# A hybrid decoder layer in fp32 on one core: norm factors' transposes, attention's last splits and the splits of loaded operands one step later, silu's table and one weight's split sooner

## The chip, the core and the metric

The kernel runs on one core of one Trainium2 chip. A core has five engines with an instruction queue each: TensorE (PE in the profile), VectorE (DVE), ScalarE (ACT), GpSimdE (POOL) and SyncE (SP), which here issues all the DMAs. They meet through semaphores. The metric is the device time of one execution in microseconds. Before the change it is 2059.78 us, the median of three runs (2059.01 to 2061.59).

## What is computed

The reference is one decoder layer on an x of 1 x 2048 x 1024 in float32. Two token mixers work side by side on the same normalised input: gated linear attention (four heads of 64 by 128) and a gated short convolution. Their outputs are concatenated, projected and added to x. A SwiGLU feed-forward part (FFN, width 2816) and a last norm follow.

```python
h = rmsnorm(x, norm1_g[l])
proj = h @ w_in[l]
p_q, p_k, p_v, p_g, p_a, c_b, c_c, c_h = jnp.split(proj, splits, axis=-1)
...
log_a = jax.nn.log_sigmoid(p_a @ w_gate_up[l] + b_gate[l]) / GATE_NORMALIZER
o = gla_chunked(q, k, v, log_a)
o = rmsnorm(o, gla_norm_g[l])
o = o * jax.nn.silu(p_g.reshape(bsz, seq, GLA_HEADS, GLA_DV))
...
o_conv = c_b * causal_depthwise_conv(c_c * c_h, conv_w[l])
mixed = jnp.concatenate([o_gla, o_conv], axis=-1) @ w_out[l]
x = x + mixed
h2 = rmsnorm(x, norm2_g[l])
ffn = (jax.nn.silu(h2 @ w_ffn_gate[l]) * (h2 @ w_ffn_up[l])) @ w_ffn_down[l]
x = x + ffn
return rmsnorm(x, norm_f_g)
```

## The kernel before

**Precision.** A product of float32 matrices is made of three matmuls. Each operand is split into a rounded upper part, hi, and the rest, lo (split, L190: hi is a copy on ACT, lo a subtraction on DVE), and product_step (L455) issues hi x hi at L460, hi x lo at L461 and lo x hi at L462. Every weight and every moving operand therefore costs one instruction on ACT and one on DVE before PE can use it.

**Products.** The input projection and the FFN work with seven block products in place of eight (a Strassen-Winograd scheme). The list PRODUCTS (L48) pairs weight blocks with operand blocks: A11 B11, S1 T1, S2 T2, A12 B21, S3 T3, S4 B22, A22 T4. One call of unit (L464) takes one weight of 1024 x 256 and does the seven products, mul(0) to mul(6), on 1024 positions. A product is 12 matmuls with 512 columns. The accumulators oa and ob (PSUM banks) are used again within a unit: mul(4) adds to oa, after ACT has copied c12 out of it (L500); L489 adds a later accumulator to a copy, on DVE. Seven split quarters of a weight go through four buffers.

**Halves.** The 2048 positions are two halves of 1024. in_proj(0) and in_proj(1) make the input projection, a unit per two blocks of columns; out_proj(0) and out_proj(1) make the output projection (L1201 to L1204); ffn_up and ffn_down follow for each half. Everything between them goes through DRAM.

**Order.** The program is traced by Python generators. A product ends in tick (L271). On every second tick it takes one step of the generator that stands first in background (more often while hurry, steady or hasty hold), and on one of four ticks one step of ahead. So a generator's yields say after how many products its next piece is traced. The tile framework then plans each engine's instructions in an order of its own, from the order of tracing and from estimated times, and the engine takes them in that order. behind(marks) and tc.issue_after(instruction) hold an instruction behind given ones. In the opening, that is, in the first quarter of the input projection up to its first whole unit, ordered is set: split_in_order (L177) and queued (L167) chain the instructions of ACT, and those of DVE, in the order in which they are written, and ticks take no step.

**The opening's first unit.** unit_weights (L418) leaves A22 unsplit while ordered is set (L451). The unit splits it at L518, after the four subtractions of T4 and their splits (difference, L730, called by rest() in two portions through then()). After that the order by hand ends.

**Loaded operands.** load_pairs (L917) gets the second half's operands of the input projection for in_proj(1), four tiles for each of the seven blocks. Four blocks were stored split and are loaded as pairs (load_pair). T3, B22 and T4 (WHOLE, L59) were stored unsplit; load_whole (L923) loads such a tile and splits it at once. load_h2 and act_op use load_whole for the FFN.

**Norm factors.** position_rstd (L217) sums squares over partitions by matmuls, makes 1/sqrt on DVE by eleven small operations (L230, L243 to L248), copies it along the free axis (rep, L234) and transposes that four times on PE into a bank (L238). h2_ahead (L1278) calls it twice at the beginning of ffn_up(0), and finish_later (L1400) twice in the second half, both as steps of ahead. combine (L328) follows in h2_ahead, with 28 steps.

**Attention.** gla_half (L1056) does 16 chunks of 128 positions by three steps each: gla_scores, gla_finish of the chunk before, gla_outputs. gla_finish (L1157) transposes the normed output of a chunk, multiplies by the gate (L1162), splits it (L193, L194) and stores both parts in s_gla. out_proj loads these as operands (build_mix, L1185).

**Tables.** ACT loads a table of functions when an instruction needs another set. finish_rstd (L252), which h2_first uses in out_proj(1), takes Ln and Exp. silu (L538) in the FFN needs its own set.

Of the kernel before, what the change touches and what calls it, by code (L numbers as in the profile page):

```python
# [20 lines left out]
P = 128  # L21
# [32 lines left out]
def tile_hymba_block(ctx, tc, x, xt, win, wa, wgu, wout, wffn, wdown, wdown_first, small, out):  # L54
# [97 lines left out]

    last_hi, last_lo, raw_loads = [], [], []
    last_out = []
# [61 lines left out]

    def position_rstd(n, *sums, into=()):  # L217

# [16 lines left out]
        ]  # L235
        for dst in (rb, *into):
            for t in range(PT):
                pe.transpose(dst[:, t * P : (t + 1) * P], rep[:, t, :], ident[:])  # L238
        return rb

# [11 lines left out]
    def finish_rstd(v, tot, n, rb=None):  # L252
        l, y0 = bt("l"), bt("y0")
        act.activation(l[:], tot[:], AF.Ln, bias=eps[:], scale=1.0 / n)
        act.activation(y0[:], l[:], AF.Exp, scale=-0.5)
        dve.tensor_scalar(v[:], tot[:], 1.0 / n, EPS, ALU.mult, ALU.add)
        newton((v if rb is None else rb)[:], v[:], l[:], y0[:])
# [206 lines left out]
    def unit(src, ops, into=None, onto=None, raw=None, between=(), rest=None):  # L464
# [43 lines left out]
        mul(2, oa)  # L508
        c12 = copied("c12", oa, (0, 1))
        o = mul(3)  # L510
        then()
        plus(c11, o)
        mul(4, oa)
        then()
        plus(c22, oa)
        if rest is not None:
            next(rest, None)
            w["A22"] = weight_quarter(w["A22"])  # L518
            held[:] = last_hi + last_lo
            ordered.clear()  # L520
        mul(5, ob)
        plus(c12, ob)
        mul(6, oa)
        if into is not None or onto is not None:
            copied("c21", oa, (1, 0))
        return [(0, 0, c11, False), (1, 1, c22, False), (0, 1, c12, False), (1, 0, oa, True)]

    def settled(c, in_psum):
# [388 lines left out]
    def load_pairs(src):  # L917
        ops = no_operands()
        for _, n in PRODUCTS:
            ops[n] = [(load_whole if n in WHOLE else load_pair)(p) for p in src[n]]  # L920
        return ops

    def load_whole(src):  # L923

        o = opp.tile([P, 2, PB], F32R, name="op", tag="op")
        load(o[:, 1, :].bitcast(F32), src[:])
        split(o[:, 1, :].bitcast(F32), o[:, 0, :], o[:, 1, :])
        return o
# [127 lines left out]
    def gla_half(half):  # L1056
# [7 lines left out]
        for n, (b, t) in enumerate(chunks):  # L1064
            cur = nxt
            s = gla_scores(b, t, *cur)
            yield
            if o is not None:
                gla_finish(*chunks[n - 1], *o)
                yield  # L1070
            if n + 1 < len(chunks):
                nxt = gla_load(*chunks[n + 1])
            o = gla_outputs(b, t, *s)
            yield
        gla_finish(b, t, *o)
        done.add((b, t))
# [80 lines left out]
    def gla_finish(b, t, osb, g):  # L1157
# [4 lines left out]
        dve.scalar_tensor_tensor(osb[:], ot[:], col(C_GN), g[:], ALU.mult, ALU.mult)  # L1162
        split(osb[:], g[:].bitcast(F32R), osb[:].bitcast(F32R))
        for e, y in enumerate((g, osb)):
# [67 lines left out]
    def h2_first(ssq, ops):  # L1232
# [5 lines left out]
        for j in range(2):  # L1238
            rb.append(tiny.tile([P, PB], F32, name="rb2", tag="rb"))
            column_rstd(ssq[j], D, rb[j])  # L1240
            yield

        def put(n, k, h):
            if n in LATER:
# [33 lines left out]
    def h2_ahead(ssq):  # L1278
# [3 lines left out]
        for j in range(2):  # L1282
            for _ in range(2):
                yield
            rb.append(position_rstd(D, ssq[j]))

# [113 lines left out]
    def finish_later(half):  # L1400

        for j in range(2):
# [6 lines left out]
            yield  # L1409
            rb = position_rstd(D, ssq)  # L1410
            for d in range(KD):
                y = bt("y")
                load(y[:], s_x1[2 * half + j][d][:])
                yield
                dve.scalar_tensor_tensor(y[:], y[:], col(C_GF + d), rb[:], ALU.mult, ALU.mult)
                store(out[2 * half + j, :, d, :], y[:])
# [222 lines left out]
```

## Time and profile before

| what | value |
|---|---|
| median of three runs | 2059.78 us (2059.01 to 2061.59) |
| profiled execution, its own time | 2056.94 us |
| span of its instructions | 2055.2 us |
| mean granted TensorE clock | 0.995 |
| instructions | 27032 |
| matmuls | 9271 |
| DMA traffic | 422.54 MB, 206 GB/s on the mean |

All rows come from that one profiled execution. A row of the timeline has the start in us from the span's start, the duration, the engine, the line, the operation with its output and input, its shape, and in brackets the engine's idle time before it and what ended that. A matmul's duration is modelled, and matmuls overlap: how fast PE goes is read from one start to the next. A row of the windows has the stretch and its length, then the busy time and the count for PE, PEld (weight loads), DVE, ACT and POOL, the granted TensorE clock, the busy share of the DMA engines and GB/s. A row of the waits has the engine, the line that waits, what it waits for, and then the total, the number and the longest.

### The profile page before, as it was taken

The numbers are of one execution on the slowest core, as the hardware profiler recorded it, in microseconds if no ns is written. First come the engines' busy times: TensorE is split into PE (matmuls) and PEld (weight loads), VectorE is DVE, ScalarE is ACT, GpSimd is POOL, SyncE is SP. The second block draws the span as 40 slices with busy tenths as digits, with TensorE's granted clock in tenths as the row PEclk, the third lists the DMA queues.
The fourth block names the chain that finished last, engine by engine and source line by source line (L and its number), as shares of the span: only waits on it lengthen the run. The fifth ranks groups of instructions, "written<-read, shape, count | busy, mean of one in ns | idle before, by whom it ended". The sixth has DMA issues, their size and how long they took to land.

```text
span 2055.2 us, 27032 instructions
## 1 busy us (share of the span) xinstructions
PE 2024.1 (98%) x9271; PEld 1664.6 (81%) x9271; DVE 1548.4 (75%) x2533; ACT 979.9 (48%) x1934; POOL 336.4 (16%) x218
## 2 busy tenths in 40 slices
PE   9999999999999999999999999999999999999997
PEld 8778878787888888888888888887888878888886
DVE  7878976569743787887786788877777777778884
ACT  6665455766543344444444552335544544453344
POOL 0000000000002451232131112201312221211213
PEclk9999999999999999999999999999999999999999
DMA  7356786425686873555454676576544534486663
GB/s 261 116 196 214 281 303 194 140 75 170 221 275 218 327 273 123 207 182 205 159 181 147 236 277 253 190 279 249 180 148 169 188 125 169 168 323 215 241 226 117
DMA packets 189738, 422.54 MB, mean 206 GB/s; under 512 B 19904, under 2 KB 65184, under 8 KB 180128
## 3 DMA queue, kind: packets, MB, share of 16 engines
q1 hardware_dynamic: 189600, 420.81, 57.8%
q8 instruction: 73, 1.20, 0.2%
q14 instruction: 65, 0.53, 0.1%
HBM read 276.02 MB, written 144.70 MB: 205 GB/s over the span
## 4 chain that ended last, share of the span: by engine, by line
PE 86%; DVE 5%; DMA 4%; ACT 3%; issue 2%; SPq 0%; POOL 0%; DVEq 0%; ACTq 0%; POOLq 0%
PE mm L460 25%; PE mm L462 24%; PE mm L461 24%; DMA op<-sa_T 2%; PE mm L1201 2%; PE mm L1202 2%; PE mm L1204 2%; DVE wq L194 1%; DMA raw<-in_wffn_dram 1%; DVE h L882 1%; PE a_ps L958 1%; PE mm L744 1%; PE mm L746 1%; PE mm L745 1%; PE o_ps L1125 1%
## 5 line engine op out<-in xcount | busy, mean ns | idle before, releaser
L460 PE MATMUL mm<-op,wq 128*128 128x512 f32 x2467 | 961.7, 393 | 13.7 <-ACT c L500 6.6
L461 PE MATMUL mm<-op,wq 128*128 128x512 f32 x2467 | 960.8, 390 | 0.2 <-DVE op L194 0.2
L462 PE MATMUL mm<-op,wq 128*128 128x512 f32 x2467 | 951.2, 390 | 0.5 <-DVE wq L194 0.2
L193 ACT ACTIVATE wq<-raw 128x512 fp32r<-128x512 f32 (+2 forms) x612 | 355.4, 587 | 588.3 <-PE mm L462 456.5
L194 DVE TENSOR_TENSOR wq<-raw,wq 128x512 fp32r<-128x512 f32 (+2 forms) x612 | 449.1, 739 | 179.7 <-ACT wq L193 177.8
L460 PEld LDWEIGHTS mm<-op,wq 128*128 128x128 f32 x2467 | 464.2, 188 | 118.2 <-ACT c L500 8.5
L462 PEld LDWEIGHTS mm<-op,wq 128*128 128x128 f32 x2467 | 464.2, 188 | 100.1 <-DVE wq L194 2.4
L461 PEld LDWEIGHTS mm<-op,wq 128*128 128x128 f32 x2467 | 464.3, 188 | 96.1 <-DVE op L194 1.3
L1183 POOL TENSOR_TENSOR ssx<-ssx,q 128x512 f32<-128x512 f32 x52 | 74.8, 1453 | 867.6 <-ACT q L1182 867.4
L489 DVE TENSOR_TENSOR c<-mm,c 128x512 f32<-128x512 f32 x196 | 134.8, 688 | 56.2 <-PE mm L462 53.7
L489 DVE TENSOR_TENSOR y<-mm,y 128x512 f32<-128x512 f32 x185 | 126.5, 687 | 47.4 <-PE mm L462 47.1
L435 DVE TENSOR_TENSOR raw<-raw 128x512 f32<-128x512 f32 (+2 forms) x192 | 151.7, 794 | 3.2
L1314 POOL TENSOR_TENSOR t<-c,c 128x512 f32<-128x512 f32 x44 | 73.9, 1678 | 432.0 <-DVE c L1310 409.7
L500 ACT ACTIVATE c<-mm 128x512 f32<-128x512 f32 x198 | 115.5, 588 | 19.0 <-PE mm L462 15.8
L1201 PE MATMUL mm<-op,wq 128*128 128x512 f32 x256 | 100.7, 395 | 0.0
L435 DVE TENSOR_TENSOR s<-raw 128x512 f32<-128x512 f32 (+2 forms) x96 | 64.1, 668 | 48.3 <-DMA raw<-in_wffn_dram 23.7
L1202 PE MATMUL mm<-op,wq 128*128 128x512 f32 x256 | 99.9, 390 | 0.0
L193 ACT ACTIVATE wq<-s 128x512 fp32r<-128x512 f32 (+2 forms) x96 | 56.2, 586 | 88.9 <-PE mm L462 85.3
L1396 POOL TENSOR_TENSOR y<-x,y 128x512 f32<-128x512 f32 x32 | 58.3, 1823 | 229.8 <-DVE y L489 163.7
L1204 PE MATMUL mm<-op,wq 128*128 128x512 f32 x256 | 79.9, 390 | 0.0
L435 DVE TENSOR_TENSOR raw<-s,raw 128x512 f32<-128x512 f32 (+2 forms) x96 | 69.8, 727 | 1.9
L194 DVE TENSOR_TENSOR op<-op 128x512 fp32r<-128x512 f32 x94 | 62.0, 686 | 5.3 <-ACT op L193 5.0
(230 smaller groups left out, 1777.4 us busy)
## 6 DMA issues: line engine op xcount, KB each, us to landing
raw<-in_wffn_dram SPq DMA_DIRECT2D x44, 1024.0 KB, 6.1
sa_B<-so SPq DMA_DIRECT2D x47, 512.0 KB, 3.4
op<-sa_B SPq DMA_DIRECT2D x47, 512.0 KB, 7.1
raw<-in_win_dram SPq DMA_DIRECT2D x22, 1024.0 KB, 5.4
sa_T<-so SPq DMA_DIRECT2D x44, 512.0 KB, 4.2
op<-sa_T SPq DMA_DIRECT2D x44, 512.0 KB, 6.6
raw<-in_wdown_dram SPq DMA_DIRECT2D x24, 768.0 KB, 5.6
sx<-y SPq DMA_DIRECT2D x48, 256.0 KB, 4.2
```

The costliest lines, as they stand in the source:

```text
L193: last_hi[:] = [act.activation(hi, src, AF.Copy)]
L194: last_lo[:] = [dve.tensor_tensor(lo, src, hi.bitcast(F32), ALU.subtract)]
L435: dve.tensor_tensor(*args)
L460: pe.matmul(o[:], wh, xh, start=first and k == 0, stop=False, skip_group_check=True)
L461: pe.matmul(o[:], wh, xl, start=False, stop=False, skip_group_check=True)
L462: return pe.matmul(o[:], wl, xh, start=False, stop=k == n - 1, skip_group_check=True)
L489: last_plus[:] = [dve.tensor_tensor(t[:], o[:], t[:], ALU.add)]
L500: last_out[:] = [act.activation(t[:], o[:], AF.Copy)]
L1183: pool.tensor_tensor(ssq[:], ssq[:], q[:], ALU.add)
L1201: pe.matmul(o[e, j][:], wh, m[:, 0, :], start=k == 0, stop=False)
L1202: pe.matmul(o[e, j][:], wh, m[:, 1, :], start=False, stop=False)
L1204: pe.matmul(o[e, j][:], wl, ops[k][j][:, 0, :], start=False, stop=k == KD - 1)
```

## The change

Six edits.

- position_rstd becomes a generator. It yields between the copy along the free axis and the transposes, and appends its result to a list. h2_ahead yields once before it and once after it for each of its two calls (before: twice ahead of it). finish_later takes one step more per call.
- gla_finish becomes a generator too. It yields after the multiplication by the gate. The split, now held behind last_out and last_plus, and the two stores are traced with the next step. gla_half drops the yield that stood behind it; its last call gives one yield more than before.
- load_undivided loads without a split. load_pairs uses it for T3, B22 and T4 and notes the tiles. due(n) in unit splits such a block's four tiles, held behind last_out: T3 after product 3 has been added, B22 after product 4, T4 after product 5. In all other units due finds nothing.
- In the opening's first unit A22 is split after c12's copy, ahead of product 3 and of T4's four; at its old place the outstanding lo is issued.
- After h2_first's two norms the table of silu is loaded (held behind the last Exp).
- load_whole is load_undivided and a split, for the callers that are left.

```diff
-    def position_rstd(n, *sums, into=()):
+    def position_rstd(n, rbs, *sums):
...
-        for dst in (rb, *into):
-            for t in range(PT):
-                pe.transpose(dst[:, t * P : (t + 1) * P], rep[:, t, :], ident[:])
-        return rb
+        yield
+        for t in range(PT):
+            pe.transpose(rb[:, t * P : (t + 1) * P], rep[:, t, :], ident[:])
+        rbs.append(rb)
...
-        act.activation(y0[:], l[:], AF.Exp, scale=-0.5)
+        last_exp[:] = [act.activation(y0[:], l[:], AF.Exp, scale=-0.5)]
...
         c12 = copied("c12", oa, (0, 1))
+        if rest is not None:
+            w["A22"] = weight_quarter(w["A22"])
         o = mul(3)
         then()
         plus(c11, o)
+        due("T3")
         mul(4, oa)
         then()
         plus(c22, oa)
+        due("B22")
         if rest is not None:
             next(rest, None)
-            w["A22"] = weight_quarter(w["A22"])
+            catch_up()
             held[:] = last_hi + last_lo
             ordered.clear()
         mul(5, ob)
         plus(c12, ob)
+        due("T4")
         mul(6, oa)
...
+    undivided = {}
+
+    def due(n):
+        for o in undivided.pop(n, ()):
+            with behind(last_out):
+                split(o[:, 1, :].bitcast(F32), o[:, 0, :], o[:, 1, :])
...
-            ops[n] = [(load_whole if n in WHOLE else load_pair)(p) for p in src[n]]
+            ops[n] = [(load_undivided if n in WHOLE else load_pair)(p) for p in src[n]]
+            if n in WHOLE:
+                undivided[n] = ops[n]
         return ops
 
-    def load_whole(src):
-
+    def load_undivided(src):
         o = opp.tile([P, 2, PB], F32R, name="op", tag="op")
         load(o[:, 1, :].bitcast(F32), src[:])
+        return o
+
+    def load_whole(src):
+
+        o = load_undivided(src)
         split(o[:, 1, :].bitcast(F32), o[:, 0, :], o[:, 1, :])
         return o
...
             if o is not None:
-                gla_finish(*chunks[n - 1], *o)
-                yield
+                yield from gla_finish(*chunks[n - 1], *o)
...
-        gla_finish(b, t, *o)
+        yield from gla_finish(b, t, *o)
         done.add((b, t))
...
         dve.scalar_tensor_tensor(osb[:], ot[:], col(C_GN), g[:], ALU.mult, ALU.mult)
-        split(osb[:], g[:].bitcast(F32R), osb[:].bitcast(F32R))
+        yield
+        with behind(last_out + last_plus):
+            split(osb[:], g[:].bitcast(F32R), osb[:].bitcast(F32R))
...
+        with tc.issue_after(last_exp[0].ins):
+            act.preload_act_table_set("silu_and_others")
+
...
-            for _ in range(2):
-                yield
-            rb.append(position_rstd(D, ssq[j]))
+            yield
+            yield from position_rstd(D, rb, ssq[j])
+            yield
...
-            rb = position_rstd(D, ssq)
+            rb = []
+            yield from position_rstd(D, rb, ssq)
...
-                dve.scalar_tensor_tensor(y[:], y[:], col(C_GF + d), rb[:], ALU.mult, ALU.mult)
+                dve.scalar_tensor_tensor(y[:], y[:], col(C_GF + d), rb[0][:], ALU.mult, ALU.mult)
```

More of the change, by code (lines that the diff above doesn't have):

```diff
@@ L151, in store @@
         return nc.sync.dma_start(dst, src)
-    last_hi, last_lo, raw_loads = [], [], []
+    last_hi, last_lo, raw_loads, last_exp = [], [], [], []
     last_out = []
```

## The prediction, made before the changed kernel was run

> **What bounds the kernel now.** I read the busy times and the chain of waits first, then the waits of TensorE alone, then the timeline around each long one, then windows for the granted clock.
>
> ```profile
> span 2055.2 us, 27032 instructions
> PE 2024.1 (98%) x9271; PEld 1664.6 (81%) x9271; DVE 1548.4 (75%) x2533; ACT 979.9 (48%) x1934; POOL 336.4 (16%) x218
> ...
> PE 86%; DVE 5%; DMA 4%; ACT 3%; issue 2%; SPq 0%; POOL 0%; DVEq 0%; ACTq 0%; POOLq 0%
> ```
>
> PE is busy for 98% and carries 86% of the chain. No edit touches a matmul of a product, so only PE's waits, and what follows them, can be won.
>
> ```profile
> PE mm L460 <- ACT c L500: 6.6, 5, 2.1
> PE mm L460 <- ACT wq L193: 3.0, 3, 1.9
> PE rb_ps L238 <- DVE rep L234: 2.3, 1, 2.3
> PE mm L460 <- ACT wq L180: 1.9, 1, 1.9
> ```
>
> The columns are the total wait, how often, and the longest. These four groups hold 13.8 us in ten waits. That is all there is to win, beside what a wait does to the matmuls after it:
>
> ```profile
> 80.48 0.39 PE L461 MATMUL mm<-op,wq 128*128 128x512 f32 x1
> 80.71 0.39 PE L462 MATMUL mm<-op,wq 128*128 128x512 f32 x1
> 83.03 0.50 PE L460 MATMUL mm<-op,wq 128*128 128x512 f32 x1 [1.93 <-ACT wq L180]
> ...
> 126.10 0.50 PE L460 MATMUL mm<-op,wq 128*128 128x512 f32 x1 [1.85 <-ACT wq L193]
> ...
> 277.18 0.50 PE L460 MATMUL mm<-op,wq 128*128 128x512 f32 x1 [2.11 <-ACT c L500]
> ...
> 278.35 0.63 PE L461 MATMUL mm<-op,wq 128*128 128x512 f32 x1
> 278.78 0.63 PE L462 MATMUL mm<-op,wq 128*128 128x512 f32 x1
> ...
> 764.83 0.50 PE L460 MATMUL mm<-op,wq 128*128 128x512 f32 x1 [0.63 <-ACT wq L193]
> ...
> 1423.57 0.50 PE L460 MATMUL mm<-op,wq 128*128 128x512 f32 x1 [1.69 <-ACT c L500]
> ...
> 1688.06 1.12 PE L238 MATMUL rb_ps<-ident,rep 128*128 128x128 f32 x4 [2.27 <-DVE rep L234]
> ```
>
> The first column is the start. Starts lie 0.23 apart as a rule (80.48 to 80.71) but 0.43 apart after the wait of 2.11 (278.35 to 278.78). The windows have the granted clock third from the end:
>
> ```profile
> 80.00:90.00 10.00, 8.07 (x28) 5.83 (x27) 8.91 (x15) 8.30 (x17) 0.00 (x0) 0.83 0.65 219
> 90.00:100.00 10.00, 10.00 (x46) 8.27 (x45) 8.08 (x16) 9.89 (x23) 0.00 (x0) 1.00 0.56 201
> 275.00:285.00 10.00, 7.89 (x28) 6.29 (x28) 6.69 (x11) 5.61 (x11) 0.00 (x0) 0.83 1.00 367
> 700.00:710.00 10.00, 10.00 (x46) 8.29 (x45) 10.00 (x9) 2.31 (x4) 7.43 (x5) 1.00 0.88 297
> 1680.00:1690.00 10.00, 7.51 (x34) 6.06 (x33) 7.15 (x22) 2.82 (x5) 0.00 (x0) 0.89 0.38 149
> 1690.00:1700.00 10.00, 10.00 (x43) 8.17 (x42) 3.57 (x6) 2.87 (x5) 0.00 (x0) 0.94 0.14 53
> ```
>
> Each of the waits of 1.93, 2.11 and 2.27 us is followed by a low clock: (1 - 0.83) x 10 = 1.7 us lost at 80 and at 275, and (1 - 0.89) x 10 + (1 - 0.94) x 10 = 1.7 us at 1688. These three waits are dear, some 3.7 us each, and three edits of the change aim at them.
>
> **Step 1, the norm factors' transposes.** One of the four calls of position_rstd stalls PE: at 1688.06 its transposes stand in PE's order ahead of a product, and rep comes late.
>
> ```profile
> 1687.59 0.42 DVE L234 COPY rep<-py 128x512 f32<-128x512 f32 x1
> ```
>
> rep ends at 1687.59 + 0.42 = 1688.01, the last of a chain of small operations that stand between splits on DVE. The new yield puts the transposes one ahead step later. Such a step is taken every fourth product; a product is 12 matmuls at 0.2275, 2.73 us, so 10.9 us later. That is far more than the 2.27 us missing: the wait and its clock loss go, -2.3 - 1.7 = **-4.0**. The end that is worst here is 0 (the transposes are placed where they were). Nothing is added. What is behind the transposes is the scaling of stored rows, spread over hundreds of us; the second half's h2_ahead starts its 28 combining steps 8 products (22 us) later, and its operands are wanted only by the second half of the FFN.
>
> **Step 2, the undivided operands of in_proj(1).** At 277.18 PE waits for ACT's copy of c12, and ACT had splits in front of it:
>
> ```profile
> 272.83 1.27 ACT L193 ACTIVATE op<-op 128x512 fp32r<-128x512 f32 x2 [1.52 <-DMA op<-siT]
> ...
> 275.50 1.14 ACT L193 ACTIVATE op<-op 128x512 fp32r<-128x512 f32 x2
> 276.54 0.58 ACT L500 ACTIVATE c<-mm 128x512 f32<-128x512 f32 x1
> ...
> 281.43 0.63 ACT L193 ACTIVATE wq<-raw 128x512 fp32r<-128x512 f32 x1 [2.05 <-DMA raw<-in_win_dram]
> ```
>
> The new code holds the twelve splits (0.63 on ACT, 0.69 on DVE each) behind c12's copy. Without the four ahead of it the copy ends over 2 us sooner. The most that can come is the wait and its clock, -2.1 - 1.7 = -3.8. But the next unit's weights only land at 281.43 with the DMA share at 1.00, and its first product began 284.39 - (281.43 + 0.63) = 2.3 us behind their first split: PE can move ahead by no more before it meets them. I take **-2.3**, nearest to that row; ends -3.8 (the loads move up too) and 0 (the splits, now late, take the place of the copy).
>
> **Step 3, A22 in the opening's first unit.** At 83.03 PE waits for A22's hi, the last on ACT's hand-written order:
>
> ```profile
> 82.36 0.61 ACT L180 ACTIVATE wq<-raw 128x512 fp32r<-128x512 f32 x1
> ...
> 89.01 0.69 ACT L993 ACTIVATE g<-z,sml 128x512 f32<-128x512 f32 x1 [0.42 <-PE z L984]
> ...
> 81.70 1.48 DVE L184 TENSOR_TENSOR op<-h,op 128x512 fp32r<-128x512 f32 x2
> 83.10 0.69 DVE L184 TENSOR_TENSOR wq<-raw,wq 128x512 fp32r<-128x512 f32 x1
> ```
>
> Moved before T4's four, its lo (0.69) is now ahead of theirs on DVE, which is full there (81.70 to 83.79 without a gap). T4's last lo then ends near 83.18 + 0.69 = 83.9, where an unstalled last product (from 80.71 + 0.23 = 80.94, 10 matmuls on, 83.2) wants it: a rest of 0.65. So at most -(1.93 - 0.65) - 1.7 = -3.0. But ACT is at 8.30 and 9.89 of 10 in the two windows from 80 on, and the wait of 1.85 at 126.10 is again one for ACT: what PE wins it waits out there, except for the time in which ACT itself waits for PE, such as 0.42 at 89.01; I put all such gaps up to 126 at 1.0, an estimate from that one. I take **-1.0**; ends -3.0 and +0.7 (one more split in T4's way, all else given back).
>
> **Step 4, silu's table.**
>
> ```profile
> 771.17 1.28 ACT L540 ACT_TABLE_LOAD   x1
> 772.46 0.63 ACT L540 ACTIVATE c<-c 128x512 f32<-128x512 f32 x1
> ```
>
> This load of 1.28 us, the first before silu in the FFN, moves from there to the output projection, where ACT has 2.31 of 10 busy (700 to 710). The wait that stands nearest, 0.63 at 764.83, comes before the load of before, so little of it is on the path: **-0.3**, ends 0 and -1.28. The Trainium skill, ScalarE: Activation LUTs, What ACT_TABLE_LOAD costs, gives 2.66 us for a switch with its drain, by which the lower end would be -2.7. This trace doesn't agree: the next ACT instruction starts 1.29 us after the load does.
>
> **Step 5, attention's last splits.** The step count per chunk stays, but the two halves end one background step later (every second product: 5.5 us). Only the end of the second half can matter, since out_proj(1) loads what it stores:
>
> ```profile
> 648.30 0.52 SPq L151 DMA_DIRECT2D sgla<-osb  x1
> ...
> 653.29 4.71 SPq L148 DMA_DIRECT2D op<-sgla  x7
> ...
> 669.79 0.39 PE L1201 MATMUL mm<-op,wq 128*128 128x512 f32 x1
> ...
> 759.12 0.69 DVE L435 TENSOR_TENSOR s<-raw 128x512 f32<-128x512 f32 x1 [2.87 <-DMA raw<-in_wffn_dram]
> ```
>
> The stores move from 648.30 to 653.8, the loads behind them on SP's queue from 653.29 to about 657.4: +4.1, since other loads use some of the gap. The cover is this: the products that use them begin at 669.79, still 12.4 us behind the first load. Behind them come h2_first's loads and DVE's full stage (10.00 of 10 at 700), which ends in gaps that wait for a weight's DMA, 2.87 at 759.12; these take up most of a shift. I take **+0.5**; ends 0 and +4.1, if that cover is gone.
>
> What this step wins is time in which ACT waits for osb. None of the four groups of PE's waits names it, so it counts 0.
>
> **Sum.** -4.0 - 2.3 - 1.0 - 0.3 + 0.5 = -7.1, from the profiled execution's 2056.94 to 2049.8. That execution is 2.84 below the median of the runs (2059.78); taken from the median the forecast is **2052.7**. A measurement of this kernel tells 0.2%, 4.1 us, from no change: faster means under 2055.7, slower over 2063.9.
>
> **Rivals.**
> - All is kept: the opening's gain isn't waited out and the loads move up. -4.0 - 3.8 - 3.0 - 0.3 = -11.1, 2048.7. For it: three clock losses go. Against: the DMA row at 281.43 and ACT at 9.89.
> - Given back: steps 2 and 3 end in the next wait, and the lag of step 5 passes on whole: -4.0 - 0.3 + 4.1 = -0.2, 2059.6. For it: DVE at 10.00 of 10 behind the loads. Against: the 12.4 us between loads and products.
> - Slower: the held splits become a series in front of products 4, 5 and 6 of in_proj(1)'s first unit. They are written behind the addition that ends each product before, and DVE may take them in that order:
>
> ```profile
> 274.68 0.39 PE L462 MATMUL mm<-op,wq 128*128 128x512 f32 x1
> ...
> 275.11 0.69 DVE L489 TENSOR_TENSOR c<-mm,c 128x512 f32<-128x512 f32 x1 [0.28 <-PE mm L462]
> ```
>
> The addition starts 0.43 behind the last matmul's start, 0.20 behind the moment at which the next product would start. With its 0.69, a hi of 0.63 and a lo of 0.69 each of the three products waits 2.2, over the 1.93 from which a clock loss of 1.7 follows here: 3 x 3.9 = 11.7, less the 3.8 of before, +7.9 in place of -2.3, so 2052.7 + 2.3 + 7.9 = 2062.9. It decides as soon as the splits stand behind the additions; one late landing among them makes it slower by more than a measurement can miss. Against: the order that is held names c12's copy alone, and T3's loads land before the wait.
> - The change doesn't do what it says: the transposes come where they were in PE's order, because the engine orders are planned from estimates. Then step 1 is 0: -3.1, 2056.7. Against: four whole products lie between now.
> - No clock loss follows a wait as such. The Trainium skill, TensorE: Matmul & The Clock Gate, Part 1: The HAM clock gate, has the array throttled only after a whole idle window of about 3.4 us, in a window that runs freely. By that rule the waits here cost their own length, and removing them wins that alone. As a mechanism of this kernel: step 1 is -2.3, the sum -2.3 - 2.3 - 1.0 - 0.3 + 0.5 = -5.4, so 2054.4. The trace speaks against it: 0.83, 0.83 and 0.89 follow waits of 1.93, 2.11 and 2.27. For it: the wait of 1.85 at 126.10 and that of 1.69 at 1423.57 are followed by full spacing.
>
> **How the numbers follow.** The forecast has a chance of 0.40 (its own range 2050 to 2055.5), all kept 0.15, no clock loss 0.03, given back 0.20, the series 0.15, no move 0.07. Faster by over 0.2%: 0.40 + 0.15 + 0.03 = 0.58. Within 0.2%: no move 0.07, 0.14 of given back and 0.08 of the series, 0.29 in all. Slower: the rest of these two, 0.06 + 0.07 = 0.13, where more waits come on top. The range reaches down to 2047, all kept with 1.7 for one of the waits that I count as untouched, and up to 2063.5, which holds the series.
>
> **What would show it.** Step 1: no wait at the transposes of L238's successor near 1685, and clock 1.00 there. Step 2: c12's copy on ACT ahead of the splits near 275, and a clock of 1.00. Step 3: A22's split ahead of T4's four, a wait under 0.7 near 81, and a longer one near 124. Step 4: no table load near 771, and one in the output projection. Step 5: op<-sgla near 657, and the FFN's first product not later against the output projection's. Waits of 2 us at products 4 to 6 near 275 to 300, or loads of op<-sgla that end PE's waits from 670 on, would prove me wrong.

## The result and the profile after

The changed kernel takes 2055.81 us, the median of eleven runs (2050.15 to 2058.08), against 2059.76 for the kernel before (2058.80 to 2063.48). The ratio is 0.9979 with a 95% interval of 0.9971 to 0.9987: some 4.3 us faster. Run a second time beside other kernels it had 0.9968 (0.9957 to 0.9980). The forecast was 2052.7, and its bound for "faster" was 2055.7: the first median lies 0.1 us outside that bound, while the interval of the ratio is clear of 1.

The first lines of the page after:

```profile
span 2048.4 us, 26987 instructions
...
PE 2021.6 (99%) x9271; PEld 1662.2 (81%) x9271; DVE 1549.0 (76%) x2533; ACT 971.7 (47%) x1930; POOL 335.4 (16%) x218
...
PE 87%; DVE 4%; DMA 4%; ACT 2%; issue 1%; SPq 1%; POOL 0%; DVEq 0%; ACTq 0%; POOLq 0%
```

The work is the same. ACT has four instructions and 8 us fewer; the four are loads of tables (19 before, 15 after). The profiled execution took 2050.15 us, 5.7 below its median, and that of before 2056.94, 2.8 below. So the two profiles show where the time went but not by how much; a second profile of the same program stands beside it below. TensorE's waits after:

```profile
PE mm L460 <- ACT c L500: 5.0, 3, 3.0
PE mm L460 <- ACT op L193: 2.1, 1, 2.1
...
PE mm L460 <- ACT wq L193: 1.2, 3, 0.5
```

Two of the four groups of before are gone: the wait for rep, and that for A22's split. That for weights has lost its 1.85. Two waits over 2 us are left, in the timeline of PE:

```profile
80.65 0.39 PE L462 MATMUL mm<-op,wq 128*128 128x512 f32 x1
80.88 0.39 PE L460 MATMUL mm<-op,wq 128*128 128x512 f32 x1
...
273.03 0.51 PE L460 MATMUL mm<-op,wq 128*128 128x512 f32 x1 [2.10 <-ACT op L193]
...
476.19 0.53 PE L460 MATMUL mm<-op,wq 128*128 128x512 f32 x1 [3.01 <-ACT c L500]
```

Near 81 PE goes on without a gap. Near 273 the wait is as long as before, and only its releaser has another name: a split of T3 in place of c12's copy. The wait of 3.01 is new. It is for the 1826th matmul with 512 columns (counted from 0). The kernel before has no wait there, but one 48 matmuls, or four products, ahead of it, for the 1778th:

```profile
469.92 0.50 PE L460 MATMUL mm<-op,wq 128*128 128x512 f32 x1 [1.11 <-DVE c L489]
```

That wait is gone, and so is one of 1.83 near 401. The windows around the two waits that went:

```profile
80.00:90.00 10.00, 9.79 (x44) 7.79 (x43) 9.91 (x18) 6.50 (x15) 0.00 (x0) 1.00 0.35 140
1680.00:1690.00 10.00, 10.00 (x45) 8.26 (x44) 4.73 (x7) 3.97 (x8) 0.00 (x0) 1.00 0.16 61
1690.00:1700.00 10.00, 10.00 (x50) 8.42 (x49) 8.90 (x24) 3.60 (x8) 0.35 (x1) 1.00 0.45 158
```

The clock, 0.83, 0.89 and 0.94 there before, is 1.00.

All kernels here issue the same 8437 matmuls of 512 columns, so they can be compared by the start of the n-th of them (from 0), read from the traces (the last row is the span):

| matmul | place | before | after | difference | after, second profile | difference |
|---|---|---|---|---|---|---|
| 288 | end of the opening | 79.12 | 79.06 | -0.06 | 79.72 | +0.60 |
| 480 | in_proj(0) | 129.49 | 124.14 | -5.35 | 124.79 | -4.70 |
| 1248 | attention's first chunks | 317.62 | 312.24 | -5.38 | 315.19 | -2.43 |
| 1824 | ahead of the wait of 3 us | 481.85 | 472.56 | -9.29 | 475.64 | -6.21 |
| 1872 | behind it | 497.12 | 492.33 | -4.79 | 495.71 | -1.41 |
| 2400 | out_proj(0) | 648.03 | 644.99 | -3.04 | 649.23 | +1.20 |
| 5712 | FFN, second half | 1407.19 | 1406.17 | -1.02 | 1412.09 | +4.90 |
| 6912 | ahead of the transposes | 1684.72 | 1681.61 | -3.11 | 1687.49 | +2.77 |
| 7008 | behind them | 1710.90 | 1704.76 | -6.14 | 1710.64 | -0.26 |
| end | | 2055.2 | 2048.4 | -6.8 | 2053.8 | -1.4 |

The change wins about 5 us in the opening's first unit and 4 at the transposes: from matmul 6880 to 7008 the kernel before takes 34.74 us, the changed one 30.40 in both profiles. (The row of 6912 shows less, because the sums of squares that belong to the transposes stand ahead of it before the change and behind it after.) Between matmuls 480 and 2400, where attention runs beside the projection, it gives back 2.3 us in the one profile (-5.35 to -3.04) and 5.9 in the other. From 2400 to 5712 it loses another 2.0 and 3.7; 1.8 and 1.7 of that lie between matmuls 3900 and 4100, where two new waits stand, of 0.63 and 0.56 near 1010.

### The profile page after: what moved, and what is told of

The parts are those of the page before. It is cut to its first block, busy times and chain, and to the rows that moved or that the text cites. A ratio compares the mean times of both kernels' runs of the same rounds, so it can differ in the third digit from the quotient of the medians.

```text
span 2048.4 us, 26987 instructions
## 1 busy us (share of the span) xinstructions
PE 2021.6 (99%) x9271; PEld 1662.2 (81%) x9271; DVE 1549.0 (76%) x2533; ACT 971.7 (47%) x1930; POOL 335.4 (16%) x218
## 4 chain that ended last, share of the span: by engine, by line
PE 87%; DVE 4%; DMA 4%; ACT 2%; issue 1%; SPq 1%; POOL 0%; DVEq 0%; ACTq 0%; POOLq 0%
PE mm L460 25%; PE mm L462 25%; PE mm L461 25%; PE mm L1220 2%; PE mm L1221 2%; PE mm L1223 2%; DMA raw<-in_wffn_dram 1%; DVE wq L194 1%; DVE h L894 1%; PE a_ps L976 1%; PE mm L756 1%; PE mm L758 1%; PE mm L757 1%; DMA raw<-in_win_dram 1%; PE o_ps L1144 1%
## 5 line engine op out<-in xcount | busy, mean ns | idle before, releaser
L552 ACT ACTIVATE c<-c 128x512 f32<-128x512 f32 x78 | 49.2, 631 | 34.7 <-DVE c L489 32.7
```

## The experiments

Five kernels undo one part of the change each; the others change the order around it. The ratios are to the kernel before, run beside it; two kernels are told apart where their intervals do not overlap.

**A22 back in its place.**

```diff
         c12 = copied("c12", oa, (0, 1))
-        if rest is not None:
-            w["A22"] = weight_quarter(w["A22"])
...
             next(rest, None)
-            catch_up()
+            w["A22"] = weight_quarter(w["A22"])
```

> The changed kernel with A22's split of the opening's first unit put back behind T4's four. The prediction's step 3 (most of it is waited out again near 124): slower than the changed kernel by 1.0 us. The theory from the two traces (both ACT waits, 1.93 at 80.7 and 1.85 at 123.9, hung on this one split, and the clock loss behind the first): slower by 4.9 us, both waits back, the clock under 0.9 from 80 to 90.

2060.70 us, ratio 0.9999 (0.9988 to 1.0010). Without this one edit nothing measurable is left of the change: it is worth 0.0020 to 0.0031 of the time, 4 to 6 us. The clock from 80 to 90 is 0.83 again, and both waits come back in PE's timeline of this kernel:

```profile
84.23 0.50 PE L460 MATMUL mm<-op,wq 128*128 128x512 f32 x1 [1.93 <-ACT wq L180]
...
127.45 0.50 PE L460 MATMUL mm<-op,wq 128*128 128x512 f32 x1 [1.83 <-ACT wq L193]
```

What ties the second to the first is ACT's timeline. In the kernel before, three table loads lie around it:

```profile
117.92 1.28 ACT L540 ACT_TABLE_LOAD   x1
122.19 1.28 ACT L1005 ACT_TABLE_LOAD   x1
126.59 1.28 ACT L540 ACT_TABLE_LOAD   x1
```

In the changed kernel there is one, and the next unit's weights are split before T4's operands:

```profile
76.44 0.61 ACT L193 ACTIVATE wq<-raw 128x512 fp32r<-128x512 f32 x1
78.42 0.63 ACT L193 ACTIVATE wq<-s 128x512 fp32r<-128x512 f32 x1 [1.36 <-PE mm L462]
78.95 1.14 ACT L180 ACTIVATE op<-h 128x512 fp32r<-128x512 f32 x2
...
119.53 1.28 ACT L552 ACT_TABLE_LOAD   x1
```

The first of those weight splits stood at 84.38 before. The order that ACT is given has changed well beyond A22 itself: idle time at 77 is filled, and two switches between the tables of silu and of the forget gates, 2.6 us, are gone. With A22 put back the three loads are there again (119.27, 123.53, 127.93), and that weight split stands at 85.58. Which of the two, the earlier split or the fewer loads, ends the second wait is not separated.

**The transposes in the step of the factors.**

```diff
-        yield
         for t in range(PT):
             pe.transpose(rb[:, t * P : (t + 1) * P], rep[:, t, :], ident[:])
         rbs.append(rb)
+        yield from ()
...
             yield
-            yield from position_rstd(D, rb, ssq[j])
             yield
+            yield from position_rstd(D, rb, ssq[j])
```

> The changed kernel with the transposes of the norm factors traced in the step in which the factors are made. The prediction's step 1: slower than the changed kernel by 4.0 us, all of it at the wait of 2.3 us near 1680. From the traces: 5.6 us come back (1.3 near 1500, 4.3 near 1680), and if the two new waits near 1010 (0.63 and 0.56) come from h2_ahead's later start, 1.8 us go, so slower by 3.8 us net; if those waits stay, 5.6.

2058.48 us, 0.9991 (0.9979 to 1.0002): 2.5 to 4.7 us slower than the changed kernel by its two ratios, though the intervals overlap. The wait is back, longer than in the kernel before (2.27):

```profile
1688.07 1.12 PE L237 MATMUL rb_ps<-ident,rep 128*128 128x128 f32 x4 [4.08 <-DVE rep L234]
```

So is the low clock behind it:

```profile
1680.00:1690.00 10.00, 5.70 (x26) 4.56 (x26) 6.63 (x21) 2.38 (x4) 0.00 (x0) 0.80 0.32 116
1690.00:1700.00 10.00, 10.00 (x40) 8.09 (x39) 2.77 (x5) 2.87 (x5) 0.00 (x0) 0.86 0.14 52
```

The waits of 0.63 and 0.56 near 1010 are gone from this profile, as the second reading has it, and matmuls 3900 to 4100 take 45.33 us, as in the kernel before, in place of 47.12. So the edit costs some 1.8 us there. It doesn't do so alone: most other kernels with the new h2_ahead have waits of up to 0.7 at these two places, but the one without the due splits and without attention's later splits, below, has none and takes 45.33 too.

**The splits of T3, B22 and T4 where they are loaded.**

```diff
-            ops[n] = [(load_undivided if n in WHOLE else load_pair)(p) for p in src[n]]
-            if n in WHOLE:
-                undivided[n] = ops[n]
+            ops[n] = [(load_whole if n in WHOLE else load_pair)(p) for p in src[n]]
```

> The changed kernel with the splits of T3, B22 and T4 put back to where they are loaded. The prediction's step 2: slower than the changed kernel by 2.3 us. From the traces (the wait for c12's copy became one of 2.10 for T3's hi, which now stands behind that copy): slower by 0.5 us, within the measurement, with the wait of about 2.1 named c12's copy again.

2054.54 us, 0.9973 (0.9963 to 0.9983), between the changed kernel's two ratios: here this part of the change moves nothing that the runs can tell. PE's wait in this kernel is again for the copy, and of the same length:

```profile
272.52 0.50 PE L460 MATMUL mm<-op,wq 128*128 128x512 f32 x1 [2.11 <-ACT c L500]
```

**Attention's splits and stores in the step of the transposes.**

```diff
         dve.scalar_tensor_tensor(osb[:], ot[:], col(C_GN), g[:], ALU.mult, ALU.mult)
-        yield
-        with behind(last_out + last_plus):
-            split(osb[:], g[:].bitcast(F32R), osb[:].bitcast(F32R))
+        split(osb[:], g[:].bitcast(F32R), osb[:].bitcast(F32R))
...
+        yield from ()
...
                 yield from gla_finish(*chunks[n - 1], *o)
+                yield
```

> The changed kernel with attention's splits and stores put back into the step of the transposes. The prediction's step 5: faster than the changed kernel by 0.5 us, at out_proj(1) or behind it. From the traces (gate(1) comes one background step later because gla_half(0) has a step more, and meets a fuller DVE near 470): faster by 2 us, the wait of 3.0 for c12's copy near 473 back to about 1.1. Rival: the wait near 473 comes from the split's own place, not from gate(1).

2051.04 us, 0.9961 (0.9947 to 0.9975), 1.4 to 3.7 us faster than the changed kernel by its two ratios; the intervals overlap. It has no wait of 3 us behind matmul 1824, and at the 1778th the wait of the kernel before:

```profile
468.44 0.50 PE L460 MATMUL mm<-op,wq 128*128 128x512 f32 x1 [1.11 <-DVE c L489]
```

**The changed kernel once more**, beside the next three.

> The changed kernel itself once more, for a second profile beside its first, which was 5.7 us below the median of its runs. If the clock's loss behind a wait depends on the moment, the profiled time comes out near the median (2054 to 2058), with the same waits and with low clocks behind other ones. If the first profile was typical, it comes out near 2050 again, with the clock at 1.00 behind the wait of 2.1 near 271.

2053.80 us (2052.10 to 2055.66). Its profiled execution took 2055.54, as the first alternative has it; but behind the wait of 2.11 near 271 the clock is 1.00 again, as the second has it. The waits of the first profile are there (3.33 near 480), and two that the first had not or hardly: 1.44 near 302, at a transpose of attention, and 1.24 near 312 (0.18 in the first), behind this instruction of ACT:

```profile
308.89 0.42 ACT L1105 ACTIVATE ee<-ee 128x256 f32<-128x256 f32 x1 [6.33 <-DMA ee<-sd]
```

ACT stands 6.3 us at the loads of attention's third chunk, 4.6 in the first profile, 1.39 in the kernel before. What stands ahead of it in SP's queue, here of this run:

```profile
300.76 0.33 SPq L148 DMA_DIRECT2D raw<-in_win_dram  x1
301.14 2.01 SPq L148 DMA_DIRECT2D kq<-sk  x4
303.20 0.90 SPq L148 DMA_DIRECT2D ee<-sd  x2
```

and of the kernel before:

```profile
294.76 3.34 SPq L148 DMA_DIRECT2D kq<-sk  x4
298.15 3.75 SPq L148 DMA_DIRECT2D ee<-sd  x2
...
308.78 1.11 SPq L148 DMA_DIRECT2D raw<-in_win_dram  x1
```

A weight's load has moved ahead of the chunk's loads, and they are issued 6.4 us later though PE is ahead (3.8 later in the first profile, behind the same load). In the kernel with A22 back in its place it stands behind them again (310.72), in those without the due splits or without attention's edit ahead (299.21 and 299.99). Here a part of the opening's gain can be given back: from matmul 480 to 1248 nothing in the first profile (-5.35 to -5.38), 2.3 us in the second. That the moved load is the cause is not shown. The kernel with A22 back in its place has it in the old order and still takes 190.7 us there, no less than the second profile (190.4).

**No table load ahead.**

```diff
-        with tc.issue_after(last_exp[0].ins):
-            act.preload_act_table_set("silu_and_others")
```

> The changed kernel without the table load behind the last Exp. The prediction's step 4: slower than the changed kernel by 0.3 us, at most 1.3, with the load of 1.28 back before the FFN's first silu. What is left over when the four single edits measured so far are added (the change makes 0.0021 of the time, A22 0.0020, the transposes 0.0012, the splits due later -0.0006, attention's -0.0018): 0.0013, or 2.7 us.

2053.54 us, 0.9969 (0.9957 to 0.9980), against 0.9968 for the changed kernel run beside it: nothing, though the load is back ahead of the first silu of the FFN, at 770.69. So the rest of 2.7 us is not this edit's. No run shows whose it is, or whether it is only what separate measurements of a ratio leave open.

**gate(1) in its old step.** gate(1) makes the forget gates of the second half, and stands behind attention's first half in background. The edit of attention stays, and the pause ahead of it is a step shorter.

```diff
-    background.extend([pause(3), hastened(gla_half(0), 14), gate(1, ops)])
+    background.extend([pause(2), hastened(gla_half(0), 14), gate(1, ops)])
```

> The changed kernel with the pause ahead of attention's first half cut from 3 background steps to 2. gate(1) comes in its old step again, while attention's splits and stores stay in a step of their own. If attention's edit costs its time because gate(1) is late: faster than the changed kernel by nearly as much as with that edit undone (4.8 us by the medians), no wait of 3 us near 473. If it costs it by the place of the splits, or at out_proj(1): within 1.5 us of the changed kernel.

2052.69 us, 0.9961 (0.9948 to 0.9975), 1.4 us below the changed kernel run beside it, not told apart: by the time alone this is the second alternative. The profile decides on the place: the wait of 3 us is gone and that of 1.11 is back, with the splits in a step of their own.

```profile
466.93 0.50 PE L460 MATMUL mm<-op,wq 128*128 128x512 f32 x1 [1.11 <-DVE c L489]
```

From matmul 1248 to 2400 this kernel takes 326.4 us (318.62 to 645.03), the changed one 332.8 and, in its second profile, 334.0. But attention's loads now begin a step sooner, and up to matmul 1248 it is 6.4 us behind the first profile of the changed kernel, with waits of 2.73 near 271 and 2.12 near 309.

**The kernel before with a pause of 4**, the same question from the other side.

> The kernel before with the pause ahead of attention's first half 4 background steps long in place of 3, and nothing of the change. gate(1) then comes one step late with the splits in their old place. If the late gate(1) makes the wait of 3 us: 3.0 to 3.8 near 478 to 485 in place of 1.1 near 468, and slower than the kernel before by 2 to 5 us. If that wait needs attention's later splits: 1.1 as before, and no slower than by 1 us.

2065.06 us, 1.0018 (1.0008 to 1.0029): 3.7 us slower, with nothing of the change in it. The wait of 1.11 is gone, and at the 1826th matmul stands one only just shorter than expected:

```profile
487.99 0.50 PE L460 MATMUL mm<-op,wq 128*128 128x512 f32 x1 [2.85 <-ACT c L500]
```

So the wait doesn't need the change. A longer or shorter pause moves the first half's chunks as well as gate(1); the order of PE tells them apart. gate(1)'s first matmul (z) is the 1700th of those with 512 columns in seven of the fourteen profiles here, and these have a wait of 1.11 or 1.12 for the 1778th and none for the 1826th. It is the 1724th, two products later, in the other seven, and these have one of 2.85 to 3.75 for the 1826th and none for the 1778th. Within each seven the first half's chunks stand in different places, and so do attention's splits. So the late gate(1), with what is queued behind it, makes the wait. Not all of the 3.7 us is that wait: another of 3.98 stands at a transpose near 300, where attention's second chunk comes a step later too. From matmul 1248 to 2400 this kernel takes 334.8 us, the kernel before 330.4.

**Neither the due splits nor attention's later splits** (the two edits above undone together).

> The changed kernel without the due splits and without attention's later splits: A22, the transposes and silu's table alone are left of the change. If the edits add: faster than the changed kernel by 1.3 + 4.8 = 6.1 us, 2049.7. If the gain of either hung on the other's place in the order: no faster than the better of the two alone, 2051.0.

2049.64 us, 0.9953 (0.9942 to 0.9965). That fits a sum of the ratios (0.9979 - 0.0006 - 0.0018 = 0.9955), but 0.9961, the better of the two alone, lies in its interval: this run doesn't tell the two alternatives apart. Against the changed kernel run beside it, it is 3.1 us faster, not 6.1.

**What holds product 4 of in_proj(1)'s first unit.** Two kernels with the pause of 2 move A22's split there. In the first, T3 is split where it is loaded. (Both diffs leave out the pause and the place where undivided is made.)

```diff
-        w["A22"] = a22 if ordered else weight_quarter(a22)
+        w["A22"] = a22 if ordered or undivided else weight_quarter(a22)
...
-        if rest is not None:
-            w["A22"] = weight_quarter(w["A22"])
+        if rest is not None or undivided:
+            with behind([] if rest is not None else last_out):
+                w["A22"] = weight_quarter(w["A22"])
...
-            ops[n] = [(load_undivided if n in WHOLE else load_pair)(p) for p in src[n]]
-            if n in WHOLE:
+            ops[n] = [(load_whole if n == 'T3' else load_undivided if n in WHOLE else load_pair)(p) for p in src[n]]
+            if n in WHOLE and n != 'T3':
```

> The changed kernel with the pause of 2 (as in the run with that edit alone), T3 split where it is loaded, B22 and T4 due as in the change, and A22 of in_proj(1)'s first unit split behind c12's copy. If the wait near 270 is long because A22's split, which waits for product 2's end, stands on ACT ahead of the copies of c22 and c12: a wait of 0.7 to 1.0 in place of 2.1 to 2.7. If T3's loads decide: still about 2.1, now named a split or a load of T3.

2048.20 us, 0.9937 (0.9925 to 0.9950). The wait is 1.78, between what the two theories gave: T3's late loads stand ahead of the copy again, as this timeline of ACT shows.

```profile
269.13 1.28 ACT L193 ACTIVATE op<-op 128x512 fp32r<-128x512 f32 x2 [2.25 <-DMA op<-siT]
...
272.42 0.60 ACT L500 ACTIVATE c<-mm 128x512 f32<-128x512 f32 x1
```

In the second, T3 is due as in the change, and A22 follows it:

```diff
+        whole = rest is None and bool(undivided)
         due("T3")
+        if whole:
+            with behind(last_hi):
+                w["A22"] = weight_quarter(w["A22"])
```

> The changed kernel with the pause of 2, all of T3, B22 and T4 due as in the change, and A22 of in_proj(1)'s first unit split behind T3's four. Product 4 then waits for product 2's end, c12's copy and one hi of T3: 1.3 to 1.6 where the pause of 2 alone had 2.73. Against the pause of 2 alone faster by 1.2 us and, where the clock drops behind that wait, by up to 2.9. If T3's place behind c12's copy costs nothing, its wait equals that of the other kernel of this call, in which T3 is split early.

2051.61 us, 0.9954 (0.9940 to 0.9967). Now nothing but the copies of c11, c22 and c12 stands on ACT ahead of T3, and the wait is 2.14, not 1.3 to 1.6:

```profile
270.85 0.60 ACT L500 ACTIVATE c<-mm 128x512 f32<-128x512 f32 x1 [3.88 <-DMA sm<-hi]
272.82 0.60 ACT L500 ACTIVATE c<-mm 128x512 f32<-128x512 f32 x1 [1.37 <-DMA sm<-c]
273.31 1.14 ACT L193 ACTIVATE op<-op 128x512 fp32r<-128x512 f32 x2
```

The copies of c22 and c12 wait for stores of the convolution's result, whose buffers they take. My theory that A22's split decides falls too: with it out of the way the stores are next. 1.2 us by the wait was forecast against the pause of 2 alone; the ratios give 1.4 (0.9961 to 0.9954), which is within the measurement.

**The pause of 2 without the due splits**, the changed kernel otherwise.

```diff
-    background.extend([pause(3), hastened(gla_half(0), 14), gate(1, ops)])
+    background.extend([pause(2), hastened(gla_half(0), 14), gate(1, ops)])
...
-            ops[n] = [(load_undivided if n in WHOLE else load_pair)(p) for p in src[n]]
-            if n in WHOLE:
-                undivided[n] = ops[n]
+            ops[n] = [(load_whole if n in WHOLE else load_pair)(p) for p in src[n]]
```

> The changed kernel with the pause of 2 and without the due splits: A22, the transposes, silu's table and attention's later splits, with gate(1) in its old step. If attention's edit is a gain once gate(1) isn't late: faster than the kernel without due splits and without attention's edit (0.9953 of before), by up to 3 us. If it isn't, equal to it. The wait near 473 is 1.1 and the one near 396 is gone.

2046.89 us, 0.9938 (0.9924 to 0.9952): with the first of the two kernels above the fastest here, 12.8 us below the kernel before, and clear of both ratios of the changed kernel. Against the kernel without attention's edit (0.9953) it is 3.1 us faster by the ratios, as expected, though those intervals overlap. The wait near 473 is 1.11 (at 463.36), and that for c12's copy near 396, which the kernel without attention's edit has (1.83 at 397.33), is gone. From matmul 1248 to 2400 it takes 326.5 us, that kernel 332.0. Whether attention's edit wins this or the shorter pause, which also starts attention sooner, is open: no run has the pause of 2 with attention's splits in their old place.

The kernel with the pause of 2 differs from this one by the due splits alone. This one is 4.7 us faster by the ratios (0.9961 to 0.9938; the intervals overlap by 0.0004), and takes 190.4 us from matmul 480 to 1248 in place of 194.0. So with that pause the due splits are not free but seem to cost time.

## Why the prediction was right in its sum and not in its terms

The forecast was -7.1 us; measured were -4.3 and, the second time, -6.6 (0.0032 of 2060). Direction and range held, and the size was of the right order. The terms did so less well: step 3 won 3 to 5 us more than forecast, and steps 2 and 5 lost about as much. That these errors cancelled is luck. By the time alone, 2055.81, two rivals lie nearer than the forecast: the one without a clock loss (2054.4) and the one in which the transposes don't move (2056.7). The traces exclude both, as told below.

**Step 1, the transposes: -4.0, and right.** The wait of 2.27 and its clock loss are gone, the stage from matmul 6880 to 7008 is 4.3 us shorter in both profiles, and the undone edit brings wait and low clock back at the same place. "Nothing is added" was wrong: the two waits near 1010, some 1.8 us, go when this edit is undone. By the times the edit is worth 2.5 to 4.7 us in all.

**Step 2, the undivided operands: -2.3 forecast, 0 measured.** What failed is "Without the four ahead of it the copy ends over 2 us sooner". Only two of the four stood between the copy and what it had to wait for. The two at 272.83 were over when A22's split, which waits for PE, could start; c22's copy stands behind that split (the kernel before):

```profile
274.49 0.63 ACT L193 ACTIVATE wq<-raw 128x512 fp32r<-128x512 f32 x1 [0.39 <-PE mm L462]
275.02 0.58 ACT L500 ACTIVATE c<-mm 128x512 f32<-128x512 f32 x1
```

The two splits at 275.50 then hold c12's copy until 276.54, 1.0 us, and in this order it couldn't gain more. The changed kernel's ACT shows what became of that:

```profile
270.36 0.63 ACT L193 ACTIVATE wq<-raw 128x512 fp32r<-128x512 f32 x1 [3.91 <-PE mm L462]
270.89 0.58 ACT L500 ACTIVATE c<-mm 128x512 f32<-128x512 f32 x1
271.87 0.60 ACT L500 ACTIVATE c<-mm 128x512 f32<-128x512 f32 x1 [0.39 <-DMA sm<-c]
272.36 1.14 ACT L193 ACTIVATE op<-op 128x512 fp32r<-128x512 f32 x2
```

A22's split waits for PE, c22's copy stands behind that split, c12's copy behind both and behind a store, and now T3's first split behind them all. The copy did come sooner: it ends 1.92 us behind the start of the last matmul ahead of the wait (270.55), against 2.44 in the kernel before (274.68). But the split that was ahead of it became the next in line. That was the end at 0 in the prediction, "the splits, now late, take the place of the copy".

**Step 3, A22: -1.0 forecast, -4 to -6 measured.** The wait at A22 was read right, and the size was off: the wait of 1.93 and the clock went without the rest of 0.65. What failed is the step "what PE wins it waits out there". I took ACT's share of 8 to 10 tenths from 80 on for a bound. But that work was itself late, because A22's split held the rest back: the next unit's first weight split moved from 84.38 to 76.44, two table loads fell away, and the second wait, of 1.85, went with the first.

**Step 4, silu's table: -0.3 forecast, 0 measured.** The load stands at 681.45 in the output projection, as foreseen, and none is near 771.

**Step 5, attention's splits: +0.5 forecast, +1.4 to +3.7 by the times, in intervals that overlap.** What failed is "Only the end of the second half can matter". The stores and loads at that end moved as foreseen, in kind: op<-sgla starts at 653.08, 2.7 us later against PE than before, and hidden. But gla_half(0) has a step more, so gate(1), next in background, comes two products later, and with it the second half's attention. On ACT a copy that PE waits for then stands behind work on the loads of the next chunk, which waits for DMA (the changed kernel):

```profile
472.76 0.63 ACT L193 ACTIVATE wq<-raw 128x512 fp32r<-128x512 f32 x1 [0.59 <-PE mm L462]
473.56 0.21 ACT L1023 ACTIVATE el<-g 128x4 f32<-128x4 f32 x1 [0.16 <-DVE g L1022]
474.79 0.42 ACT L1105 ACTIVATE ee<-ee 128x256 f32<-128x256 f32 x1 [1.02 <-DMA ee<-sd]
...
475.56 0.58 ACT L500 ACTIVATE c<-mm 128x512 f32<-128x512 f32 x1
```

The window of that place has the low clock behind the wait:

```profile
470.00:480.00 10.00, 6.99 (x25) 5.29 (x24) 10.00 (x22) 4.24 (x10) 0.00 (x0) 0.83 0.50 133
```

DVE is at 10.00 there, but it is so in the kernel before too, so a full DVE alone doesn't make the wait. On balance the waits of 1.83 near 401 and of 1.11 near 470 go, and 0.68 near 385, 3.01 and 1.7 us of clock come. The two runs with another pause, and the place of gate(1) in all profiles, show the cause. With gate(1) in place the edit may itself be a gain; that is not shown.

"That is all there is to win" left out PE's smaller waits for DVE, of which one, 1.11, went; and it left out that a new wait can come, as 3.01 did.

Of the rivals, the series at products 4 to 6 did not come: T3's splits cost one wait, not three. The lag of step 5 was not passed on by the loads. The rival in which the transposes don't move falls by the profile: they stand at the 7000th matmul, seven products behind their old place (four were forecast). The rival without a clock loss is answered below.

What stays open is the exact share of each edit, since the intervals of single kernels are 3 to 6 us wide and the two measurements of the changed kernel differ by 2, and why the wait near 1385, for an addition on DVE, lies between 0.06 and 2.71 from profile to profile.

## What to carry to other kernels

A generator that gets one more yield delays everything queued behind it by a step: count its steps, and look at what the next in the queue will then meet. An engine that is full behind a late instruction doesn't prove that the gain at that instruction will be given back; ask whether its work was late for the same reason. Before you take work from in front of a waiting copy, list everything that the copy waits for (its buffer's last store too): the next of these may end only a moment sooner.

## What the runs showed of the hardware

The same wait can be followed by a low clock or not. Near 271, in the same order of PE's work, waits of 2.10 and 2.11 were followed by 1.00 in both profiles of the changed kernel. With the splits of T3, B22 and T4 undone, a wait of 2.11 at the same place was followed by 0.94 and 0.89 (265 to 275 and 275 to 285), and in the kernel before by 0.83. Near 480 a wait of 3.01 was followed by 0.83, one of 2.85 (the pause of 4) by 1.00. So the 1.7 us that I added to each wait of about 2 us is a price that is paid in some executions and not in others.

What decides it can be read from the traces. In narrow windows the low clock turns out to be a spell of 3.41 us at 0.50, which loses 1.7 us (two such spells in a row behind a few waits). In each trace the spells start whole multiples of 3.41 us apart: in the kernel before at 83.48, 278.04 and 1687.74, that is, 57 and 413 lengths of 3.413 apart. On this grid the place near 271 looks as follows, in the kernel before:

```profile
274.63:278.04 3.41, 1.30 (x6) 0.74 (x6) 3.05 (x6) 3.41 (x7) 0.00 (x0) 1.00 1.07 413
278.04:281.45 3.41, 3.41 (x10) 2.65 (x9) 1.53 (x3) 1.32 (x4) 0.00 (x0) 0.50 1.04 380
```

and in the changed kernel:

```profile
268.32:271.73 3.41, 2.62 (x12) 1.84 (x10) 0.69 (x2) 1.12 (x2) 0.00 (x0) 1.00 1.05 402
271.73:275.14 3.41, 1.89 (x7) 1.34 (x8) 2.73 (x6) 3.27 (x7) 0.00 (x0) 1.00 1.03 409
275.14:278.55 3.41, 3.41 (x17) 2.83 (x16) 3.41 (x7) 2.11 (x4) 0.00 (x0) 1.00 0.75 226
```

Before, the whole wait lies in one stretch of the grid, in which PE is idle for 3.41 - 1.30 = 2.11 us, and the next stretch is at 0.50. After, an edge of the grid cuts the wait into 0.79 and 1.52, and the clock stays at 1.00. The wait of 2.85 is cut too, into 1.07 and 1.78. In all fourteen profiles, without their first 10 and last 15 us, PE is idle for 1.92 us or more in 22 stretches, and each time the next one is at 0.50. Of 25 stretches with 1.6 to 1.9 us five are followed by 0.50, and with less only one, which is itself at 0.50. So a gap costs clock when enough of it falls into one stretch of the grid. This rule is inferred from the traces; no run moves the grid against the work.

The free run and the length of the window fit the Trainium skill's page TensorE: Matmul & The Clock Gate, Part 1: The HAM clock gate; its figure of a whole idle window of about 3.4 us doesn't fit, since 1.92 us of idle time in one window were enough here. The rival without a clock loss, which rests on that figure, falls with it.

The clock is not why one profiled execution lay 5.7 us off the median of its runs. The second profile of the same kernel, 5.4 us longer, has the higher mean granted clock (0.997, against 0.996), and so has the run at the median, 2055.81 (0.997). What differs between the two are waits, above all those near 302 and 312, and a start 0.7 us later.
